# A two-layer transformer block on one core: both score tiles of a shared bank ahead of their passes, compressed scores and norms spread among dense steps, SBUF tiles at multiples of 128 bytes

## The chip, the core and the metric

One core of a Trainium2 chip runs the whole program in one launch. TensorE (PE) multiplies, VectorE (DVE) and ScalarE (ACT) do the elementwise work and the exponentials, GpSimd (POOL) does a few scalings, SyncE (SP) issues the DMAs. The metric is the device time of one execution in microseconds, as the median of several runs.

## The reference

Two transformer blocks run one after the other on one sequence of 512 tokens with a model width of 1024 in fp32. The first block is a gated FFN, then a mixer (sparse attention in the NSA manner with a compressed branch and two further branches, a gated convolution, attention to a memory of other tokens, merged by gates), then a second FFN. The second block has two layers, stick-breaking attention and "forgetting" attention, each followed by a gated FFN and a gated per-layer embedding. The two attentions that the change touches compute, for 16 heads of 64:

```python
# forgetting attention, per block of queries (second_block, layer 2)
logits = einsum('bhqd,bhkd->bhqk', qb, k) * scale + fb[..., :, None] - f_cum[:, :, None, :]
probs  = softmax(where(kpos <= tpos, logits, -inf), axis=-1)
out    = einsum('bhqk,bhkd->bhqd', probs, v)
# k and q are rms-normed per head; f_cum = cumsum(log_sigmoid(hs @ w_f + b_f))

# NSA mixer: o = g_cmp * attn(q, compressed k, v) + g_a * attn_a(q, k_a, v_a) + g_b * attn_b(q, k_b, v_b)
# with a relative bias per head and gates g = sigmoid(h @ w_g)
```

## The kernel before

All matrix products are fp32 split into a high and a low part, so that one product of 128 rows by 128 columns by 512 tokens is three matmuls (`mm3`). A dense projection of one 128-wide slice of outputs from 1024 inputs is eight such triples, 24 matmuls of 512 columns; in the kernel's words one triple is a *step* and eight steps are a *job*. A job fetches its weights (SP's queue, 512 KB), ACT makes the high part `wh`, DVE the low part `wl`; the pool `wp` keeps three sets, so the fetch runs a job or two ahead. `h0h`, `h0l` ... are the high and low parts of the normed activations, `u..` those of the FFN's hidden layer, `m..` those of an attention's output.

The program runs in stages, in the order of time: an FFN (90 to 426 us), memory attention (to 563), the NSA mixer (`nsa`, 563 to 1157), its merge (to 1235), an FFN (to 1545), stick-breaking attention (1600 to 1905), an FFN with the embedding (to 2310), forgetting attention (`forget`, pool "fox", to 2650), and a last FFN with the embedding. In an FFN every matmul is a step of a dense job.

An attention is worked in *units*, one head and one branch at a time (32 units in `nsa`, 16 in `forget`). In `unit_scores` the 512 by 512 scores are made in four tiles of 128 queries, of which tile i has (i+1)*128 keys. Tiles 0 and 1 share one PSUM bank (256 columns each, tag "s"), tiles 2 and 3 have one each; tag "s" has two banks. After each tile a *pass* on DVE (`softmax_rows`) adds the bias and takes the extremum per row, and ACT takes the exponential. Two dense steps stand ahead of tile 3. POOL scales the rows (`unit_scale`). In the next round `unit_turn` transposes the unit's probabilities on PE (tag "t"), ACT and DVE split them into `pth` and `ptl`, and `unit_out` multiplies them with V (tag "o").

So a unit is a chain across PE, DVE, ACT and POOL, and what keeps PE busy meanwhile are dense steps. `begin(jobs)` sets up a list of jobs, `feed(n)` emits n steps of it, `pace(upto)` emits steps until a count is reached. In the loop over units `upto` rises evenly, so the steps are spread evenly over what is left of them. While `self.pinned` is set, PE keeps the order in which the code is written; else the scheduler may move instructions.

In `nsa` before its loop stand, as plain code: the queries' and keys' projections, the values, gates, head norms, `compress` (a generator of the compressed keys and values) and the compressed scores `nsa_cmp` (16 DMAs fetch a bias into `cp`, PE adds scores, transposes, softmax on DVE, ACT and POOL, transposed back). `nsa_cmp` has three parts, divided by `yield`. In the loop the second half of the queries is normed at u = 9 to 12, and two more `nsa_cmp` run at u = 13 to 15.

In `forget` a list of jobs `lead(u)` makes K, Q and V of four heads; `head_stats` and `head_norm` norm them, and `doubled` and `stacked` write the split halves `hv` and copy them with DMAs into `kd`, `kl`, `qs`, from which the scores are multiplied. A norm's matmuls multiply `hrh`, `hrl` with `selr` into tag "s". Line numbers below are those of the kernel before: L184 is a matmul, L189 a transpose, L203 and L213 the split's high and low part, L626 the pass, L628 the exponential, L1081 and L1097 are in `nsa_cmp`, L417 in `head_norm`, L477 and L478 in `fold_halves`, L1341 in `forget`.

Of the kernel before, what the change touches and what calls it, by code (L numbers as in the profile page):

```python
# [16 lines left out]
P = 128  # L17
# [145 lines left out]
class Net:  # L163
    def __init__(self, ctx, tc, a, out):
# [4 lines left out]
        self.tags = self.TAGS = ("d", "s", "t", "o")  # L169
        self.sb = ctx.enter_context(tc.tile_pool(name="sb", bufs=1))  # L170
# [396 lines left out]
    def constants(self):  # L567
# [12 lines left out]
        sq = self.t(sb, NSQ * P, "nrq", 2)[:, : 4 * P]  # L580
# [36 lines left out]
    def softmax_rows(self, pool, src, n, bias, stat, tag, bufs):  # L617

        nc = self.nc
        m = self.t(pool, 1, tag + "m", 8)  # L620
# [252 lines left out]
    def unit_scores(self, pool, b, q, k, bias, mask=None):  # L873

        st = self.t(pool, NT, "st", 4)
        pr, sc = [], {}
        both = self.bank("s")
        for i in range(NT):
            n = (i + 1) * P
            w = max(n, 256)  # L880
            qi = slice(i * P, (i + 1) * P)
            if i == 3:
                self.feed(2)
            sc = both[:, 256 * i : 256 * i + 256] if i < 2 else self.bank("s")
            self.scores(sc[:, :w], b, q, k, qi, slice(0, w), False, True, mask is None)
            if mask is not None:
                self.mm(sc[:, qi], self.ident_b, mask, start=False, stop=True)
            pr.append(self.softmax_rows(pool, sc[:, :n], n, bias(n), st[:, i : i + 1], f"pr{i}", 2))
        return pr, st
# [27 lines left out]
    def nsa(self):  # L917
        nc, tc = self.nc, self.tc
        with self.pool("nsa", "right") as pool:
# [7 lines left out]
            for cb in range(2):  # L927
                def evac(i, ps, cb=cb):
                    g = slice(4 * cb, 4 * cb + 4)
                    self.split(V[:, i, g, 0], V[:, i, g, 1], ps[:, :256].rearrange("p (g d) -> p g d", d=64), rT[:, i : i + 1])  # L930
                    if i % 2:
                        next(comp, None)
                self.dense_tok(self.a["w_v"][cb], self.h, NT, evac)

            G = self.t(pool, NT * 48, "G").rearrange("p (i c) -> p i c", c=48)
            pg = self.dbank()
            self.dense(pg, self.a["w_g"][0], self.h)
            gt = self.t(pool, S, "cv", 4)
            nc.vector.tensor_tensor(gt, pg, self.rB, op=ALU.mult)
            nc.scalar.activation(gt, gt, AF.Tanh, scale=0.5)  # L940
            nc.vector.tensor_scalar(gt, gt, 0.5, 0.5, op0=ALU.mult, op1=ALU.add)
            tp = self.bank("t")
            for i in range(NT):
                nc.tensor.transpose(tp[:, i * P : (i + 1) * P], gt[:, i * P : (i + 1) * P], self.ident)
            nc.vector.tensor_copy(G, tp.rearrange("p (i c) -> p i c", c=P)[:, :, :48])
            nc.vector.tensor_scalar(G[:, 0, :16], G[:, 0, :16], self.col("valid"), None, op0=ALU.mult)
# [4 lines left out]
            for j in range(4):  # L951
                ps = self.dbank()
                self.dense(ps, self.a["w_kv"][4 + j], self.h)
                k = self.t(pool, S, f"kx{j}") if j % 2 else self.t(pool, S, "cv", 4)
                nc.vector.tensor_tensor(k, ps, self.rB, op=ALU.mult)
                ks.append(k)
                next(comp, None)
            for _ in comp:
                pass
            st = self.head_stats(ks, self.sel64, 1)  # L960
            for j in range(4):
                self.head_norm(ks[j], j, 1, st, self.col("kg"))
# [464 lines left out]
```

## Time and profile before

| what | value |
|---|---|
| median of 3 runs | 3084.95 us (3083.20 to 3086.88) |
| the profiled execution | 3091.85 us |
| its span, first to last instruction | 3090.1 us |
| PE busy | 2950.9 us, 95% of the span |
| DVE, ACT, POOL busy | 1632.7, 1223.0, 245.7 us |
| chain that ended last, share of PE | 68% |
| DMA queue 1, share of 16 engines' span | 35.6% |
| HBM over the span | 100 GB/s |

The profiled execution was one of the runs on the chip with the recorder on. PE's busy time counts a matmul from its start to a modelled end, and successive matmuls overlap, so 95% busy is not 95% of what PE could do. The view by windows gives the busy time of each engine in a stretch; the view of waits gives, per releasing instruction, how long an engine was idle before an instruction that this release let go.

### The profile page before, as it was taken

The numbers are of one execution on the slowest core, as the hardware profiler recorded it, in microseconds if no ns is written. First come the engines' busy times: TensorE is split into PE (matmuls) and PEld (weight loads), VectorE is DVE, ScalarE is ACT, GpSimd is POOL, SyncE is SP. The second block draws the span as 40 slices with busy tenths as digits, with TensorE's granted clock in tenths as the row PEclk, the third lists the DMA queues.
The fourth block names the chain that finished last, engine by engine and source line by source line (L and its number), as shares of the span: only waits on it lengthen the run. The fifth ranks groups of instructions, "written<-read, shape, count | busy, mean of one in ns | idle before, by whom it ended". The sixth has DMA issues, their size and how long they took to land.

```text
span 3090.1 us, 37192 instructions
## 1 busy us (share of the span) xinstructions
PE 2950.9 (95%) x13873; PEld 2384.8 (77%) x13874; DVE 1632.7 (53%) x2718; ACT 1223.0 (40%) x2078; POOL 245.7 (8%) x361
## 2 busy tenths in 40 slices
PE   8999999997988999999999999999999888999999
PEld 7888887875766778888888877888877666788887
DVE  7434345674666655443348775343366555644334
ACT  6322234352554544222236564222243454422223
POOL 0000000001223320000000000000013321000000
PEclk9999999998999999999999999999999898999999
DMA  7322342343232235223343345223334334522332
GB/s 234 105 96 90 105 129 86 95 125 104 72 105 81 79 129 180 91 93 94 108 127 102 100 120 177 96 91 94 90 125 120 91 86 140 166 91 95 91 95 95
DMA packets 133230, 339.20 MB, mean 110 GB/s; under 512 B 17415, under 2 KB 30215, under 8 KB 133048
## 3 DMA queue, kind: packets, MB, share of 16 engines
q1 hardware_dynamic: 132376, 335.49, 35.6%
q10 hardware_dynamic: 672, 1.32, 0.4%
q8 instruction: 109, 1.79, 0.2%
q14 instruction: 73, 0.60, 0.1%
HBM read 279.82 MB, written 28.61 MB: 100 GB/s over the span
## 4 chain that ended last, share of the span: by engine, by line
PE 68%; DVE 6%; issue 3%; DMA 3%; ACT 2%; POOL 1%; SPq 0%; DVEq 0%; POOLq 0%; ACTq 0%
PE d L184 25%; PE s L184 14%; PE o L184 13%; PE t L184 11%; PE t L189 2%; DVE wl L213 1%; ACT wh L203 1%; DVE pr L626 1%; DMA xd<-qk 1%; DMA qk<-xd 1%; DVE ptl L213 0%; PE s L1246 0%; PE o L1256 0%; PE t L1246 0%; DVE cv L809 0%
## 5 line engine op out<-in xcount | busy, mean ns | idle before, releaser
L203 ACT ACTIVATE wh<-raw 128x1024 fp32r<-128x1024 f32 (+3 forms) x499 | 493.2, 989 | 1238.5 <-PE d L184 330.2
L213 DVE TENSOR_TENSOR wl<-raw,wh 128x1024 fp32r<-128x1024 f32 (+3 forms) x499 | 573.7, 1150 | 317.4 <-ACT wh L203 303.3
L893 POOL TENSOR_SCALAR pr<-pr,st 128x128 f32<-128x128 f32 x192 | 111.6, 599 | 331.3 <-DVE st L1341 142.2
L213 DVE TENSOR_TENSOR ptl<-t,pth 128x512 fp32r<-128x512 f32 x144 | 85.3, 596 | 32.9 <-ACT pth L203 30.1
L203 ACT ACTIVATE pth<-t 128x512 fp32r<-128x512 f32 x144 | 74.6, 521 | 70.1 <-PE t L189 69.7
L626 DVE CUSTOM_DVE_ANT_0 pr<-s,tb 128x128 f32<-128x128 f32 (+3 forms) x128 | 60.3, 488 | 72.9 <-PE s L184 51.3
L225 POOL TENSOR_TENSOR raw<-raw,cols 128x1024 f32<-128x1024 f32 x25 | 50.6, 2025 | 557.3 <-DMA xd<-x 477.9
L189 PE MATMUL t<-idn,pr 128*128 128x128 f32 x480 | 79.7, 282 | 4.7 <-DVE ptl L213 3.6
L189 PEld LDWEIGHTS t<-idn,pr 128*128 128x128 f32 x480 | 61.9, 145 | 25.4 <-DVE ptl L213 6.5
L184 PE MATMUL o<-ptl,V 128*128 128x512 f32 x192 | 59.8, 323 | 9.2 <-DVE ptl L213 8.7
L184 PE MATMUL s<-kd,qs 128*128 128x256 f32 (+1 forms) x64 | 28.5, 446 | 36.8 <-DMA qs<-hvl 20.1
L402 POOL MEMSET hrh<- 128x512 f32 (+2 forms) x10 | 4.7, 472 | 666.7 <-DVE wl L213 485.0
L184 PE MATMUL d<-h0h,wh 128*128 128x512 f32 x136 | 57.0, 419 | 0.1
L184 PE MATMUL d<-h7h,wh 128*128 128x512 f32 x136 | 56.9, 418 | 0.0
L512 ACT ACTIVATE ta<-ta 128x512 f32<-128x512 f32 x88 | 55.6, 633 | 3.0 <-DVE ta L511 2.9
L184 PE MATMUL d<-h2h,wh 128*128 128x512 f32 x136 | 56.5, 416 | 0.0
L184 PE MATMUL d<-h4h,wh 128*128 128x512 f32 x136 | 56.4, 414 | 0.0
L184 PE MATMUL d<-h6h,wh 128*128 128x512 f32 x136 | 56.3, 414 | 0.0
L184 PE MATMUL d<-h5h,wh 128*128 128x512 f32 x136 | 56.2, 413 | 0.0
L184 PE MATMUL d<-h3h,wh 128*128 128x512 f32 x136 | 55.9, 411 | 0.0
L184 PE MATMUL d<-h1h,wh 128*128 128x512 f32 x136 | 55.6, 409 | 0.0
L184 PE MATMUL o<-pth,V 128*128 128x512 f32 x192 | 55.5, 322 | 0.0
(2173 smaller groups left out, 8749.5 us busy)
## 6 DMA issues: line engine op xcount, KB each, us to landing
raw<-in_f_in_dram SPq DMA_DIRECT2D x176, 512.0 KB
raw<-in_f_out_dram SPq DMA_DIRECT2D x64, 512.0 KB
raw<-in_f_out_dram SPq DMA_DIRECT2D x32, 384.0 KB
raw<-in_w_mg_dram SPq DMA_DIRECT2D x24, 512.0 KB
raw<-in_w_cv_dram SPq DMA_DIRECT2D x24, 512.0 KB
xd<-x SPq DMA_DIRECT2D x32, 256.0 KB
x<-xd SPq DMA_DIRECT2D x32, 256.0 KB
raw<-in_w_pg_dram SPq DMA_DIRECT2D x16, 512.0 KB
```

What stands on the lines that cost most here:

```text
L184: i = self.nc.tensor.matmul(out, lhs, rhs, **kw)
L189: i = self.nc.tensor.transpose(out, src, self.ident)
L203: nc.scalar.activation(h, src, AF.Copy, scale=1.0 if scale is None else scale)
L213: eng.tensor_tensor(lo, src, hb, op=ALU.subtract)
L225: nc.gpsimd.tensor_tensor(v, v, gain.unsqueeze(2).to_broadcast([P, gain.shape[1], n]), op=ALU.mult)
L402: nc.gpsimd.memset(z.bitcast(F32), 0.0)
L512: nc.scalar.activation(ta, ta, AF.Silu)
L626: nc.vector.tensor_tensor_reduce(out=p, in0=src, in1=bias, op0=ALU.add, op1=ALU.min, scale=1.0, scalar=3e38, accum_out=m)
L893: self.nc.gpsimd.tensor_scalar(pr[i], pr[i], st[:, i : i + 1], 1.0, op0=ALU.mult, op1=ALU.mult)
```

## The change

There are five edits.

1. `unit_scores`: the tiles run in the groups (0, 1), (2), (3). Within a group all matmuls stand ahead of all passes, so that tile 1 is multiplied ahead of the pass on tile 0.
2. `nsa`: the keys' projections, the values and the gates become jobs of the list (47 jobs instead of 40, so 392 steps in all, with 16 in each `values` job, instead of 320). The head norms, the parts of `compress` and the first two `nsa_cmp` stand between feeds. `pinned` is set later, once step 104 is reached or passed. In the loop the second part of the last `nsa_cmp` comes a unit later.
3. `forget`: the list of jobs starts ahead of the small projection `w_ff` and of the transposes; of each four heads K and Q come first and V last; V has two buffers instead of three; the norms of a head pair come at u % 4 of 2 and 3, two units or more ahead of their use and after `forget_out`, instead of right before it; the pacing aims at 176 steps at u = 9.
4. `halves`: the tile pair `hv` has two buffers in `stick` and `forget`, still one in `nsa`.
5. `t()` rounds a tile's width in SBUF up to a multiple of 128 bytes, and a tile `edge` of 96 bytes per row is put at the right side; the four tiles of row extrema share one tag `sm`; the gates' transposes go through `tr`.

The instruction counts stay about the same (PE 13941 rows in the order before, 13942 in the order after).

```diff
+        self.edge = ctx.enter_context(tc.tile_pool(name="edge", bufs=1, side="right"))
+        self.edge.tile([P, 24], F32, name="edge", tag="edge")
...
     def t(self, pool, cols, tag, bufs=None, dt=F32, parts=P):
         self.uid += 1
-        return pool.tile([parts, cols], dt, name=f"{tag}_{self.uid}", tag=tag, bufs=bufs)
+        w = cols if pool is self.ps else -(-cols // 64) * 64 if dt == BF16 else -(-cols // 32) * 32
+        x = pool.tile([parts, w], dt, name=f"{tag}_{self.uid}", tag=tag, bufs=bufs)
+        return x if w == cols else x[:, :cols]
...
-        h, lo = self.pair(pool, "hv", bufs=1)
+        h, lo = self.pair(pool, "hv", bufs=self.hv)
...
-        for i in range(NT):
-            n = (i + 1) * P
-            w = max(n, 256)
-            qi = slice(i * P, (i + 1) * P)
-            if i == 3:
+        for tiles in ((0, 1), (2,), (3,)):
+            if tiles == (3,):
                 self.feed(2)
-            sc = both[:, 256 * i : 256 * i + 256] if i < 2 else self.bank("s")
-            self.scores(sc[:, :w], b, q, k, qi, slice(0, w), False, True, mask is None)
...
-            pr.append(self.softmax_rows(pool, sc[:, :n], n, bias(n), st[:, i : i + 1], f"pr{i}", 2))
+            sc = {i: both[:, 256 * i : 256 * i + 256] if i < 2 else self.bank("s") for i in tiles}
+            for i in tiles:
+                w = max((i + 1) * P, 256)
+                qi = slice(i * P, (i + 1) * P)
+                self.scores(sc[i][:, :w], b, q, k, qi, slice(0, w), False, True, mask is None)
...
+            for i in tiles:
+                n = (i + 1) * P
+                pr.append(self.softmax_rows(pool, sc[i][:, :n], n, bias(n), st[:, i : i + 1], f"pr{i}", 2))
...
-            jobs = [query(0, r) for r in range(4)] + self.conv(0, pool) + self.conv(1, pool)
+            jobs = [key(j) for j in range(4)] + [query(0, r) for r in range(4)] + [values(0), self.job(self.a["w_g"][0], self.h, gates), values(1)]
+            jobs += self.conv(0, pool) + self.conv(1, pool)
...
+            for k in range(4):
+                self.feed(8)
+                next(comp)
+            st = self.head_stats(ks, self.sel64, 1, fill=2)
+            self.feed(6)
+            for j in range(4):
+                self.head_norm(ks[j], j, 1, st, self.col("kg"))
+                self.feed(2)
...
             for b in range(2):
-                for _ in self.nsa_cmp(pool, 0, b, [qn[0, r] for r in range(4)], kc, G, pc):
-                    self.feed(5)
-            base, total = self.steps, 8 * len(jobs)
+                next(cmps[b])
+                self.feed(6)
+                for _ in cmps[b]:
+                    pass
+                if b == 0:
+                    next(cmps[1])
+                self.feed(6)
+            self.pace(8 * 12 + 8)
+            self.pinned = True
+            base = self.steps
...
+            self.begin(jobs)
+            self.feed(16)
             ps = self.dbank()
             self.dense(ps, self.a["w_ff"][0], self.h, gs)
...
-                jobs = [self.values(pool, self.a["w_fv"][u], rT, V, u, gs, 3)]
...
+                return jobs + [self.values(pool, self.a["w_fv"][u], rT, V, u, gs)]
...
-                if u % 4 == 3 and u < 15:
-                    kq[t + 1] = norm(t + 1, hst)
...
-                if u % 4 == 2 and u < 14:
-                    self.pace(48 * (u // 4 + 2))
+                if u % 4 == 1 and u < 13:
+                    self.pace(48 * (u // 4 + 1) + 32)
                     hst = self.head_stats(xs[u // 4 + 1], self.sel64, 1, pool=pool, tag="o", fill=2)
-                elif u % 4 == 0 and 0 < u < 16:
-                    kq[t + 1] = norm(t + 1, hst)
+                elif u % 4 in (2, 3) and u < 12:
+                    n = 2 * (u // 4) + u % 4
+                    kq[n] = norm(n, hst)
```

How PE's order moves is seen at three places. The first is a unit in the loop of `nsa`, from the scores' first tile to the fourth. The `s` tiles are the score banks (`s_6436` holds tiles 0 and 1), `k1d`, `k1l` and `q1s` keys and queries, `d<-h..,wh` dense steps. Before:

```order
L184 MATMUL s_6436<-k1l_993_5384,q1s_1066_5700 128x256
L184 MATMUL s_6436<-k1d_1024_5542,q1s_1066_5700 128x256 [waits DVE_49]
L184 MATMUL s_6436<-k1l_993_5384,q1s_1066_5700 128x256
L184 MATMUL s_6449<-k1d_1024_5542,q1s_1066_5700 128x384
L184 MATMUL s_6449<-k1l_993_5384,q1s_1066_5700 128x384
L184 MATMUL d_6431<-h1h_75,wh_6327 128x512
L184 MATMUL d_6431<-h1l_76,wh_6327 128x512
L184 MATMUL d_6431<-h1h_75,wl_6328 128x512
L184 MATMUL d_6431<-h2h_77,wh_6327 128x512
L184 MATMUL d_6431<-h2l_78,wh_6327 128x512
L184 MATMUL d_6431<-h2h_77,wl_6328 128x512
L184 MATMUL s_6462<-k1d_1024_5542,q1s_1066_5700 128x512 [waits DVE_49]
```

and now:

```order
L189 MATMUL s_6335<-k1l_834_4516,q1s_1012_5334 128x256
L189 MATMUL s_6335<-k1d_948_5015,q1s_1012_5334 128x256
L189 MATMUL s_6335<-k1l_834_4516,q1s_1012_5334 128x256
L189 MATMUL s_6348<-k1d_948_5015,q1s_1012_5334 128x384
L189 MATMUL s_6348<-k1l_834_4516,q1s_1012_5334 128x384
L189 MATMUL d_6330<-h1h_79,wh_6227 128x512
L189 MATMUL d_6330<-h1l_80,wh_6227 128x512
L189 MATMUL d_6330<-h1h_79,wl_6228 128x512
L189 MATMUL d_6330<-h2h_81,wh_6227 128x512
L189 MATMUL d_6330<-h2l_82,wh_6227 128x512
L189 MATMUL d_6330<-h2h_81,wl_6228 128x512
L189 MATMUL s_6361<-k1d_948_5015,q1s_1012_5334 128x512 [waits DVE_49,PE_49]
```

The second matmul of tile 0 stands first in each piece. Tile 1's first matmul has lost its wait on DVE. Tile 3's first matmul, behind the same six dense matmuls, still waits on DVE.

The second place is the border between two units of `forget`, where the keys `kd` and queries `qs` change to the next head pair. Before:

```order
L184 MATMUL o_19840<-pth_19800,V_18760 128x256 [waits Activation_49]
L184 MATMUL o_19840<-ptl_19801,V_18760 128x128
L184 MATMUL o_19840<-pth_19800,V_18760 128x128
L184 MATMUL s_19853<-kd_3739_19782,qs_3743_19794 128x256 [waits DMAHW2_49,DMAHW1_49,DMAHW0_49]
L184 MATMUL s_19853<-kl_3513_18690,qs_3743_19794 128x256 [waits DMAHW3_49]
L184 LDWEIGHTS bfc_148
L184 MATMUL s_19853<-bfc_148 128x128
L184 MATMUL s_19853<-kd_3739_19782,qs_3743_19794 128x256 [waits DVE_49]
L184 MATMUL s_19853<-kl_3513_18690,qs_3743_19794 128x256
L184 LDWEIGHTS bfc_148
L184 MATMUL s_19853<-bfc_148 128x128
```

and now:

```order
L189 MATMUL o_19570<-ptl_19530,V_18921 128x128
L189 MATMUL o_19570<-pth_19529,V_18921 128x128
L189 MATMUL s_19583<-hrh_19469,selr_151 128x512
L189 MATMUL s_19583<-hrl_19470,selr_151 128x512
L189 MATMUL s_19587<-hrh_19469,selr_151 128x512
L189 MATMUL s_19587<-hrl_19470,selr_151 128x512
L189 MATMUL s_19614<-kd_3604_19106,qs_3608_19117 128x256 [waits DMAHW6_49,DMAHW4_49,DMAHW7_49,DMAHW3_49,DVE_49]
L189 MATMUL s_19614<-kl_3502_18634,qs_3608_19117 128x256 [waits DMAHW0_49]
L189 LDWEIGHTS bfc_152
L189 MATMUL s_19614<-bfc_152 128x128
L189 MATMUL s_19614<-kd_3604_19106,qs_3608_19117 128x256
L189 MATMUL s_19614<-kl_3502_18634,qs_3608_19117 128x256
```

Before, the scores stand right behind the unit's output and wait for three DMA queues. Now a norm for a later head pair (`hrh`, `hrl` with `selr`) stands between, in two score banks, and the scores wait among others on DVE.

The third place is the second compressed scores ahead of or in the loop of `nsa`: `cp` is transposed into `t`, goes through its softmax on DVE, ACT and POOL, and is transposed back. Before, its second transposes (those that wait on Pool) follow 15 dense matmuls behind the first ones, of which the last three are here:

```order
L184 MATMUL d_5930<-h3h_79,wh_5840 128x512
L184 MATMUL d_5930<-h3l_80,wh_5840 128x512
L184 MATMUL d_5930<-h3h_79,wl_5841 128x512
L189 MATMUL t_5943<-idn_144,cp_5862 128x128 [waits Pool_49]
L189 MATMUL t_5943<-idn_144,cp_5862 128x128 x3
```

and now:

```order
L189 MATMUL s_5938<-k1d_948_5015,q0s_1000_5290 128x512 [waits DVE_49]
L189 MATMUL s_5938<-k1l_834_4516,q0s_1000_5290 128x512
L194 MATMUL t_5757<-idn_148,cp_5697 128x128 [waits DMAHW4_49,DMAHW3_49,DMAHW5_49,DMAHW2_49,DMAHW6_49,DMAHW1_49,DMAHW7_49,DMAHW0_49,DVE_49]
L194 MATMUL t_5757<-idn_148,cp_5697 128x128 x3
L194 MATMUL t_5799<-idn_148,cp_5697 128x128 [waits Pool_49]
L194 MATMUL t_5799<-idn_148,cp_5697 128x128 x3
L194 MATMUL t_5959<-idn_148,pr_1094_5845 128x128 [waits DVE_49,PE_49]
L194 MATMUL t_5959<-idn_148,pr_1096_5849 128x128
L194 MATMUL t_5959<-idn_148,pr_1099_5856 128x128
L194 MATMUL t_5959<-idn_148,pr_1106_5876 128x128
```

Now the second transposes stand right behind the first, with no dense step between, and behind the scores of the loop's second unit.

## Rows read from the trace of the kernel before

**Rows 1.** The page: its first lines, busy time of each engine.

```profile
span 3090.1 us, 37192 instructions
...
PE 2950.9 (95%) x13873; PEld 2384.8 (77%) x13874; DVE 1632.7 (53%) x2718; ACT 1223.0 (40%) x2078; POOL 245.7 (8%) x361
...
```

**Rows 2.** Windows by stage: busy us (x instructions) per engine, granted clock, DMA share.

```profile
...
563.00:700.00 137.00, 129.88 (x705) 106.57 (x704) 97.28 (x197) 57.24 (x81) 7.90 (x16) 1.00 0.40 120
700.00:770.00 70.00, 52.28 (x191) 38.96 (x190) 32.08 (x55) 19.04 (x30) 9.36 (x8) 0.83 0.35 99
770.00:1157.00 387.00, 346.90 (x1743) 280.93 (x1742) 241.51 (x556) 193.53 (x440) 112.35 (x154) 0.98 0.31 92
...
2310.00:2330.00 20.00, 15.70 (x98) 12.88 (x97) 16.96 (x25) 9.16 (x14) 7.35 (x7) 0.91 0.36 119
2380.00:2650.00 270.00, 222.54 (x1126) 175.12 (x1125) 160.65 (x336) 131.50 (x285) 58.29 (x80) 0.90 0.38 109
...
```

**Rows 3.** Waits of PE in nsa's loop, 770 to 1157: total, times, longest.

```profile
...
PE s L184 <- DVE pr0m L626: 22.7, 31, 1.6
PE o L184 <- DVE ptl L213: 8.2, 9, 1.9
PE t L189 <- DVE ptl L213: 3.1, 5, 1.7
PE t L189 <- DVE cp L1081: 3.0, 1, 3.0
...
```

**Rows 4.** Waits of PE in forget, 2310 to 2650.

```profile
...
PE s L184 <- DMA qs<-hvl: 20.1, 5, 5.4
PE s L184 <- DVE pr0m L626: 16.3, 15, 3.9
PE s L184 <- DVE st L1341: 5.2, 2, 3.1
...
PE s L184 <- DVE hrl L213: 1.6, 3, 1.3
...
PE s L184 <- DVE hrh L207: 1.2, 1, 1.2
...
```

**Rows 5.** Waits of PE ahead of nsa's loop, 563 to 770.

```profile
...
PE t L189 <- POOL cp L1097: 5.2, 2, 3.0
...
```

**Rows 6.** Timeline of a unit in nsa: start, length, engine, idle before and releaser.

```profile
...
812.96 0.28 PE L184 MATMUL s<-k1d,q1s 128*128 128x256 f32 x1
...
813.08 0.28 PE L184 MATMUL s<-k1l,q1s 128*128 128x256 f32 x1
...
814.87 0.39 PE L184 MATMUL s<-k1d,q1s 128*128 128x256 f32 x1 [1.51 <-DVE pr0m L626]
...
```

**Rows 7.** Timeline of the border between two head pairs in forget.

```profile
...
2512.96 0.28 PE L184 MATMUL o<-pth,V 128*128 128x128 f32 x1
2513.27 0.59 ACT L477 ACTIVATE on<-o 64x512 f32<-64x512 f32 x1 [1.22 <-PE o L184]
2513.90 0.68 DVE L478 TENSOR_TENSOR on<-o,on 64x512 f32<-64x512 f32 x1 [1.39 <-ACT on L477]
...
```

**Rows 8.** Windows inside long dense runs, PE alone: up, down, merge's projection.

```profile
...
154.00:174.00 20.00, 20.00 (x88) 1.00 0.28 84
345.00:365.00 20.00, 20.00 (x88) 1.00 0.42 115
1185.00:1205.00 20.00, 20.00 (x90) 1.00 0.68 251
...
```

**Rows 9.** Timeline of the second compressed scores.

```profile
...
755.36 0.63 PE L189 MATMUL t<-idn,cp 128*128 128x128 f32 x4 [1.47 <-DVE cp L1081]
...
760.55 1.05 POOL L1097 TENSOR_TENSOR cp<-cp,cz 128x512 f32<-128x512 f32 x1 [0.25 <-DVE cz L1096]
...
761.66 1.12 PE L189 MATMUL t<-idn,cp 128*128 128x128 f32 x4 [2.17 <-POOL cp L1097]
...
```

**Rows 10.** Window around the longest wait in forget, PE alone.

```profile
...
2514.00:2528.00 14.00, 8.87 (x33) 0.63 0.21 52
...
```

More of the change, by code (lines that the diff above doesn't have):

```diff
@@ L926, in nsa, with values, evac, gates @@
             V = self.t(pool, NT * 1024, "V", dt=F32R).rearrange("p (i g z d) -> p i g z d", g=8, z=2, d=64)
-            for cb in range(2):
-                def evac(i, ps, cb=cb):
+            def values(cb):
+                def evac(i, ps):
                     g = slice(4 * cb, 4 * cb + 4)
                     self.split(V[:, i, g, 0], V[:, i, g, 1], ps[:, :256].rearrange("p (g d) -> p g d", d=64), rT[:, i : i + 1])
-                    if i % 2:
-                        next(comp, None)
-                self.dense_tok(self.a["w_v"][cb], self.h, NT, evac)
+                return self.job_tok(self.a["w_v"][cb], self.h, NT, evac)
             G = self.t(pool, NT * 48, "G").rearrange("p (i c) -> p i c", c=48)
[L936 to L946, printed above, removed]
+            def gates(pg):
+                gt = self.t(pool, S, "cv", 4)
+                nc.vector.tensor_tensor(gt, pg, self.rB, op=ALU.mult)
+                nc.scalar.activation(gt, gt, AF.Tanh, scale=0.5)
+                nc.vector.tensor_scalar(gt, gt, 0.5, 0.5, op0=ALU.mult, op1=ALU.add)
+                tp = self.bank("t")
+                for i in range(NT):
+                    self.tr(tp[:, i * P : (i + 1) * P], gt[:, i * P : (i + 1) * P])
+                nc.vector.tensor_copy(G, tp.rearrange("p (i c) -> p i c", c=P)[:, :, :48])
+                nc.vector.tensor_scalar(G[:, 0, :16], G[:, 0, :16], self.col("valid"), None, op0=ALU.mult)
             kc = [self.t(pool, 4 * P, f"kc{z}", dt=F32R) for z in range(4)]
@@ L950, in nsa, with key, post @@
             ks = []
[L951 to L962, printed above, removed]
+            def key(j):
+                def post(ps):
+                    k = self.t(pool, S, f"kx{j}") if j % 2 else self.t(pool, S, "cv", 4)
+                    nc.vector.tensor_tensor(k, ps, self.rB, op=ALU.mult)
+                    ks.append(k)
+                return self.job(self.a["w_kv"][4 + j], self.h, post)
             los = [self.zeroed(pool, f"k{br}")[0] for br in range(2)]
@@ L1018, in nsa @@
                     next(cmp0)
-                elif u == 15:
-                    next(cmp1)
                 if rows:
@@ L1041, in nsa @@
                 elif u == 15:
+                    next(cmp1)
+                    kn[1] = keys(1, 1)
+                elif u == 16:
                     next(cmp1, None)
-                    kn[1] = keys(1, 1)
                 self.pace(upto)
@@ L1336, in forget @@
                 t, b = u // 2, u % 2
[L1337 to L1338 removed]
+                upto = base + (176 - base) * (u + 1) / 10 if u < 10 else 176 + 46 * (u - 9) / 7
                 if u < 16:
```

69 lines of the change are left out of this document (39 added, 30 removed).

## The prediction, made before the changed kernel ran

> **What bounds the kernel now.** I read the page first. PE is busy 95% of a span of 3090.1 us, DVE 53%, ACT 40% [rows 1]; PE is the engine that sets the end, so a gain must come from PE's idle time or from matmuls that take less. The profiled execution took 3091.85 us, 1.75 us more than its span; all sums below are made against it. The median of the three runs is 3084.95, which is 6.9 lower, and I take the same 6.9 off at the end.
>
> Then I asked by windows where PE isn't busy. Inside the long dense runs 20 of 20 us are busy at clock 1.00 [rows 8]. What is idle lies in the two attentions with filler: ahead of the loop of `nsa` 137.0 - 129.88 + 70.0 - 52.28 = 24.8 us, in its loop 40.1, at the start of `forget` 4.3 of 20, in the rest of it 47.5 [rows 2]. That is 117 us, and the change's edits 1 to 4 lie in these stretches. The view of waits then names what ended that idle time [rows 3 to 5].
>
> **Edit 1, tile 1 ahead of the pass on tile 0.** In the loop of `nsa` PE's wait for that pass costs 22.7 us in 31 times [rows 3], in `forget` 16.3 in 15 [rows 4]. The idle time is counted from the modelled end of the matmul before. Unhindered, a 256-column score matmul follows the one before at 813.08 - 812.96 = 0.12 us though each is 0.28 long [rows 6]; so a wait also loses the overlap of 0.16. This makes 22.7 + 31 x 0.16 = 27.7 and 16.3 + 15 x 0.16 = 18.7, together 46.4. In the new order tile 1 has no wait. Late next is tile 3, which takes the bank that tiles 0 and 1 shared, and waits for the pass on tile 1. Between stand tile 2 and six dense matmuls, about 1.7 us; the two passes now begin one tile later (two matmuls, 0.24 us) and are in sum under 1 us. So tile 3 finds its bank free except where DVE is held by something longer; I count 0.05 us per unit, 48 units, 2.4 back. Sum: -44. Bounds: -46.4, and -20 if tile 3 gets back more than half of it.
>
> **Edit 2, ahead of the loop.** Of the 24.8 us, the named waits are the chains of code that had no steps beside them; the largest kind is the compressed scores' wait for POOL, 5.2 in two [rows 5]. With steps in between most go. Two things come back. The second compressed scores' transposes now stand right behind each other. Their softmax chain runs on DVE, ACT and POOL from 755.36 + 0.63 to 761.66, 5.7 us [rows 9]; before, 15 dense matmuls covered most of it, and now nothing does, so 5.7 us. The first scores and the remaining short waits I count at 5, two waits of 2.5 or their like. Sum: -24.8 + 5.7 + 5 = -14. Bounds: -24.8, and +2: three chains of 5.7 uncovered, 17.1, and 10 of the old waits left. The 16 DMAs that fill `cp` wait on SP for the first scores to be done with the tile, and weights are queued behind them; `wp` holds two jobs more, 11 us of steps, so I count nothing for it.
>
> **Edit 2, in the loop.** The list is longer, so of it some 272 steps are left for 32 units by my count of the order, 8.5 in each, where there were 244, 7.6. The 0.9 step more is 0.9 x 3 matmuls of about 0.23 us, 0.6 us of cover per unit. It stands against waits for `ptl` of 8.2 + 3.1 us in 14 times [rows 3], 0.8 each. Each could lose 0.6, 8.4 in all; as the step isn't always put between transposes and output, I take half, -4.5 (bounds 0 and -8.4). The wait for `cp` in the loop, 3.0 [rows 3], gets a unit more: -2 (0 and -3). The steps themselves cost nothing new: they are the same matmuls that stood ahead of the loop. What it costs DVE: 241.5 us busy in the loop of 387 [rows 2], 62%; with 28 steps, 3.5 jobs, more in it and some 45 us less of time it comes to 71%, still not the bound.
>
> **Edit 3.** At the start of `forget` 4.3 us are idle [rows 2]; two jobs' steps now stand ahead of the small projection, -4 (0 and -4.3). In the loop the queries' DMAs cost 20.1 us in five waits; the norm's waits for score banks and for `hrh`, `hrl` cost 5.2 + 1.6 + 1.2 = 8.0 [rows 4]. The norms now come two units ahead, so the DMAs have a whole unit, 270 / 16 = 17 us [rows 2]; the second buffer of `hv` (edit 4) takes away the wait of one norm's split for the other's DMAs. 28.1 go. What is new: six norms in the loop stand right behind the unit's output and take both score banks, and the next unit's tile 0 waits for the norm's pass on DVE, which is queued behind the output's own `on`. That chain: the last output matmul ends at 2512.96 + 0.28 = 2513.24, `on` on ACT and then DVE ends at 2513.90 + 0.68 = 2514.58 [rows 7], the norm's pass on 512 columns is another 0.7 like `on`, so PE waits 2.0 us, six times 12. No dense step stands between. Sum: 12 - 28.1 = -16. Bounds: -28, and +2 if the passes on the next tile 0, queued behind the norm's three splits of 0.7 each, hold up tile 3 as well and the wait is 5 us a time. The V buffer that goes is needed again only after the units that read it: nothing.
>
> **The clock.** Where PE waits long, the granted clock falls: 0.63 in 2514 to 2528, around the longest wait of 5.4 us, where 33 instructions took 14 us [rows 4, 10]. The means are 0.83 in 700 to 770, 0.98, 0.91 and 0.90 [rows 2]. Had PE been the bound all that time, busy x (1 - clock) would be given back: 8.9 + 6.9 + 1.4 + 22.3 = 39.5. Much of what ran slowly only met its next wait sooner or later, and the new waits of 2 to 6 us will bring some of it back: I take a fifth, -8 (0 and -39.5).
>
> **Edit 5.** No row shows the same tile at another address. What the rows show is that dense runs of one form differ: 88 matmuls in 20 us where `h` or `u` moves, 90 where merge's `m` does, all at clock 1.00 and with PE never idle [rows 8]. That is 227.3 against 222.2 ns by these counts, 5.1 ns each, with one count more or less 2.5 to 7.7. In the built program merge's `m` and its `wh` start at the same residue modulo 512 bytes, while `h` or `u` and `wh` do not; with the new widths `u` and `wh` share one (384), `h` (256) and `wh` still don't. If that relation is the cause, `u`'s 4 x 8 x 22 x 3 = 2112 matmuls gain 10.8 us. It rests on one run that differs, so I take two thirds, -7. Bounds: 0, and some 8700 moving matmuls of `h` and `u` x 5.1 = -44.
>
> The Trainium skill speaks against this term: in "TensorE: Matmul & The Clock Gate", "Step-by-step: what each phase is for", the moving and the stationary operand have a read port each, and "Loading the next tile's weights doesn't steal SBUF read bandwidth from the running matmul", so addresses of one against the other shouldn't matter. By that rule the term is 0 and the time 7 us later; the trace's 90 against 88 doesn't agree by itself.
>
> **Sum.** -44 - 14 - 4.5 - 2 - 4 - 16 - 8 - 7 = -99.5; 3091.85 - 99.5 = 2992.35, less 6.9 is 2985.
>
> **Rivals.**
> *The waits only move.* PE is released from tile 1 and meets tile 3, the norms' passes and the uncovered `cp` chain at their bounds: -20 + 2 - 2 + 2 = -18, with nothing from clock or addresses. For it speaks that a unit is one chain over four engines, each of which was waiting; against, that DVE is busy only 62% in the loop [rows 2]. Time 3085 - 18 = 3067; halfway to the forecast is 3026.
> *All dense matmuls run at the rate of merge's.* -44 instead of -7: 2948. For it speaks the one run at 90; against, that only `u` gets the relation which that run has.
> *The edits don't do what they say.* If the scheduler or the pools put the same waits back, the time stays 3085. Against it stands the new order itself, in which tile 1 has no wait.
> *Slower, by the clock.* Each of 48 units now has its wait at tile 3, behind the dense steps. If that wait, or the one after the norm, is as long as those of `forget` now, the clock falls in each unit, as around 2514 [rows 10]. PE's 346.9 + 222.5 = 569 us busy in both loops stand at a mean near 0.95 now [rows 2]; at mean c they take 569 x (0.95/c - 1) more. The forecast's gain is used up at c = 0.81; at 0.78 it is +124, so 3085 - 100 + 124 = 3109. Against it: tile 3's cover of 1.7 us is longer than the two passes.
>
> **Chances.** The forecast, with the terms near their taken values (2960 to 3010): 0.60. Dense matmuls at merge's rate: 0.10. Waits that move in part or whole: 0.22. No change: 0.03. Slower by the clock: 0.05. A measurement can tell about 0.2%, 6 us, from no change. So faster 0.91, same 0.04 (the third rival and the edge of the first), slower 0.05. The range goes from 2935 (the second rival with some more clock) to 3040 (the first, three quarters of it).
>
> **What would show it.** Right: no row of waits "s <- DVE pass" at tile 1, tile 3's in its place under 3 us in sum; no wait for `qs<-hvl` in `forget`, waits of about 2 us six times for the norm's pass; one wait near 5.7 us for `cp` from POOL near the loop's start; clock over 0.95 in `forget`; `u` at 90 per 20 us and `h` at 88. Wrong: tile 3 waiting half a microsecond in most units; a weights fetch ending PE's idle time; 88 everywhere in the long runs (the addresses do nothing), or 90 everywhere.

## The result, and the profile after

The changed kernel takes 2971.41 us (median of 4 runs, 2970.22 to 2973.13) where the kernel before took 3085.91 (median of 4, 3083.20 to 3090.15) beside it: a ratio of 0.9628, 95% interval 0.9612 to 0.9645, 114.5 us less. The forecast was 2985 with a range of 2935 to 3040.

The page of the changed kernel's profiled execution, busy time of each engine over the span, answers to [rows 1]:

```profile
span 2971.2 us, 37172 instructions
...
PE 2898.9 (98%) x13873; PEld 2369.6 (80%) x13874; DVE 1628.5 (55%) x2718; ACT 1216.9 (41%) x2078; POOL 247.9 (8%) x361
...
```

The span is 118.9 us shorter, PE's busy time 52. So a bit more than half of the gain, 67 us, is PE's idle time that went, and the rest is time in which PE counts as busy: matmuls at a higher clock, or at the same clock from a better place, and overlaps that a wait had broken.

The windows of the same places of the program (busy us and instructions of each engine, granted clock) answer to [rows 2]: ahead of the loop of `nsa`, its loop, and `forget`'s start and loop.

```profile
...
559.00:696.00 137.00, 123.06 (x644) 99.73 (x644) 94.37 (x183) 58.69 (x81) 6.91 (x14) 1.00 0.40 119
696.00:722.00 26.00, 23.24 (x134) 19.64 (x134) 19.21 (x41) 8.05 (x14) 3.19 (x2) 0.97 0.50 145
...
722.00:1105.00 383.00, 365.63 (x1863) 302.08 (x1862) 255.79 (x583) 200.37 (x456) 116.69 (x158) 0.98 0.35 102
2247.00:2267.00 20.00, 17.67 (x72) 12.98 (x71) 17.41 (x19) 8.50 (x11) 10.28 (x10) 1.00 0.37 121
2267.00:2307.00 40.00, 38.26 (x207) 32.03 (x205) 29.95 (x38) 17.96 (x26) 13.28 (x8) 0.96 0.43 122
2307.00:2507.00 200.00, 186.59 (x1091) 151.43 (x1090) 143.89 (x305) 116.91 (x263) 63.24 (x76) 0.98 0.45 126
...
```

Ahead of the loop of `nsa` PE is idle for 16.7 us (24.8 before), in the loop for 17.4 of 383 (40.1 of 387 before), and in that of `forget` for 13.4 of 200 (47.5 of 270, a window that ends some 20 us behind the last scores), where the granted clock is 0.98 instead of 0.90.

The waits of PE, in the loop of `nsa` (first fence, answers to [rows 3]) and in `forget` (second, to [rows 4]): total, times, longest. `sm` is the tile of row extrema that a pass writes, formerly `pr0m` and so on.

```profile
...
PE t L194 <- POOL cp L1128: 4.7, 1, 4.7
PE s L189 <- DVE sm L631: 4.0, 5, 1.0
PE t L194 <- DVE cp L1112: 3.6, 2, 2.9
PE t L194 <- DVE ptl L218: 2.3, 3, 1.4
PE o L189 <- DVE ptl L218: 1.7, 2, 1.2
...
```

```profile
...
PE s L189 <- DVE x L422: 5.2, 9, 2.1
PE s L189 <- DVE sm L631: 4.2, 4, 1.9
PE o L189 <- DVE ptl L218: 3.9, 7, 1.1
...
```

No tile 1 waits any more. What is left of the pass is 4.0 + 4.2 us: in `nsa` three times at tile 2 and twice at tile 3, in `forget` four times at tile 3. The queries' DMAs are gone from the list in `forget`; the norm's pass (`x`, L422) has come in for 5.2, and the wait for `ptl` has grown from 0.5 + 0.5 to 3.9. In `nsa`, the 4.7 for `cp` from POOL is the compressed scores' chain, which stood ahead of the loop before and now lies in it.

Where the time went, by the stretches of the program, from the starts of the first and last matmuls of each in the traces (us; the columns of the experiments are explained below):

| stretch | before | after | unit scores alone | widths alone | nsa alone | forget alone |
|---|---|---|---|---|---|---|
| four FFN second halves, sum | 490.3 | 477.9 | 490.3 | 477.9 | 489.8 | 490.3 |
| end of FFN 1 to first unit of nsa | 324.4 | 290.1 | 325.2 | 326.2 | 290.1 | 324.0 |
| units of nsa | 352.3 | 338.3 | 321.8 | 351.6 | 372.1 | 351.7 |
| end of FFN 3 to first unit of forget | 134.5 | 117.2 | 134.4 | 133.8 | 134.7 | 118.6 |
| units of forget | 243.5 | 199.5 | 219.1 | 240.6 | 239.8 | 221.8 |
| behind them to FFN 4's second half | 278.6 | 284.0 | 278.2 | 277.2 | 278.2 | 284.1 |
| whole span | 3090.1 | 2971.2 | 3035.4 | 3070.6 | 3068.1 | 3058.1 |

A stretch that an edit doesn't touch moves by up to 4 us from one execution to the next (units of `forget` in the column "nsa alone"), so smaller differences say nothing.

### The profile page after: what moved, and what is told of

Read it like the earlier page. It is cut to its first block, busy times and chain, and to the rows that moved or that the text cites. A ratio compares the mean times of both kernels' runs of the same rounds, so it can differ in the third digit from the quotient of the medians.

```text
span 2971.2 us, 37172 instructions
## 1 busy us (share of the span) xinstructions
PE 2898.9 (98%) x13873; PEld 2369.6 (80%) x13874; DVE 1628.5 (55%) x2718; ACT 1216.9 (41%) x2078; POOL 247.9 (8%) x361
## 4 chain that ended last, share of the span: by engine, by line
PE 72%; DVE 5%; issue 3%; ACT 1%; DMA 1%; POOL 0%; SPq 0%; DVEq 0%; POOLq 0%; ACTq 0%
PE d L189 27%; PE s L189 14%; PE o L189 14%; PE t L189 12%; PE t L194 2%; DVE wl L218 1%; DVE cv L814 1%; DMA qk<-xd 0%; DVE ptl L218 0%; DMA xd<-qk 0%; PE s L1278 0%; PE o L1288 0%; PE t L1278 0%; PE o L1289 0%; ACT wh L208 0%
## 5 line engine op out<-in xcount | busy, mean ns | idle before, releaser
L633 ACT ACTIVATE pr<-pr,sm 128x128 f32<-128x128 f32 x192 | 106.0, 553 | 64.1 <-DVE sm L631 63.6
L518 DVE TENSOR_TENSOR ta<-s,ta 128x512 f32<-128x512 f32 x22 | 15.2, 692 | 74.6 <-PE s L189 74.6
L518 DVE TENSOR_TENSOR ta<-t,ta 128x512 f32<-128x512 f32 x22 | 15.2, 692 | 74.1 <-PE t L189 74.0
L482 ACT ACTIVATE on<-o 64x512 f32<-64x512 f32 x48 | 28.6, 595 | 65.8 <-PE o L189 51.1
```

The lines of the kernel that those rows point to most:

```text
L482: self.nc.scalar.activation(dst[h], po[64:], AF.Copy)
L518: nc.vector.tensor_tensor(ta, pb, ta, op=ALU.mult)
L633: nc.scalar.activation(p, p, AF.Exp, bias=m, scale=-1.0, accum_out=stat)
```

## The experiments

**One edit at a time.** Four kernels, each the kernel before with one group of edits.

```diff
 e1_unit:  before + edit 1 (unit_scores of the changed kernel)
 e5_width: before + edit 5 (t(), edge, sm, sq)
 e2_nsa:   before + edit 2 (nsa's body)
 e34_fox:  before + edits 3 and 4 (forget's body, hv buffers)
```

> The kernel before with edit 1 alone (both score tiles of a bank multiplied ahead of their passes). Theory, the wait for the pass on tile 0 was the loss and is not replaced: 31 waits in nsa and 15 in forget go, 44 us faster, some 27 of it between the start of the compressed scores and the merge and some 17 in forget, and tile 3 waits under 3 us in sum in each of the two. Rival, the unit is one chain and the wait moves to tile 3 or to ptl: 20 us faster or less, with tile 3 waiting half a microsecond in most units.

Measured 3037.15 us, ratio 0.9836 (0.9821 to 0.9850). The units of `nsa` are 30.5 us shorter, those of `forget` 24.4. PE's waits in the loop of `nsa` in this kernel:

```profile
...
PE o L184 <- DVE ptl L213: 9.3, 10, 1.9
PE t L189 <- DVE ptl L213: 5.8, 6, 2.0
...
PE s L184 <- DVE pr1m L626: 1.1, 2, 0.8
...
```

The pass's 22.7 us [rows 3] became 1.1, and `ptl` went from 11.3 to 15.1. So some 4 us moved to the next wait in the chain, and the rest was gained; the rival falls. In `forget` tile 3 waits 1.4 us in this kernel, twice. `forget` got more than its waits' 17 us, with the granted clock going from 0.90 to 0.95:

```profile
...
2360.00:2585.00 225.00, 194.68 (x1066) 155.37 (x1065) 142.69 (x308) 116.97 (x264) 56.74 (x77) 0.95 0.40 114
...
```

> The kernel before with edit 5 alone (tile widths rounded to 128 bytes, the edge tile, the shared tag sm). Theory, a 512-column matmul is faster when its moving tile and the weights loaded beside it start at the same residue modulo 512 bytes: only the FFNs' second halves gain, 2112 matmuls by 5 to 6 ns, 11 to 13 us, 3 in each FFN; the stages with h moving stay. Rival 1, a multiple of 128 bytes is what counts, as the rounding says: h gains as well, 40 us or more. Rival 2, two read ports, addresses do nothing: within 3 us of before.

Measured 3074.62 us, ratio 0.9957 (0.9942 to 0.9972). Each FFN's second half takes 119.5 us instead of 122.5 or 123.0, as in the changed kernel, and the other stretches of the table don't move beyond what executions differ by. The theory holds so far, and both rivals fall: `h` doesn't gain, and the 12 us by the medians are not nothing.

> The kernel before with edit 2 alone (nsa's keys, values and gates as jobs, norms and compressed scores between feeds, the unit's scores as before). Theory, the steps cover waits ahead of the loop and the longer list covers ptl in it: 20 us faster (14 ahead of the loop, 6 in it); nothing outside nsa moves. Rival, the steps taken out from ahead of the loop and the uncovered softmax chain of cp leave new holes: under 8 us.

Measured 3070.80 us, ratio 0.9946 (0.9931 to 0.9961). Ahead of the units it gains 34.3 us, and in the units it loses 19.8. 28 steps of 0.70 us went from ahead of the units, 27 of them into the units by the trace, 18.9 us; so the gain ahead is 34.3 - 19.6 = 14.7 net, and the units gain nothing. The waits in the loop show why:

```profile
...
PE s L184 <- DVE pr0m L626: 26.3, 32, 2.3
PE t L189 <- POOL cp L1120: 5.4, 1, 5.4
PE s L184 <- DVE pr1m L626: 3.6, 4, 1.6
PE o L184 <- DVE ptl L213: 3.0, 2, 1.9
PE t L189 <- DVE ptl L213: 1.0, 3, 0.5
...
```

`ptl` fell from 11.3 to 4.0, and the 3.0 for `cp` from DVE [rows 3] are gone. Two things took that back: the passes rose by some 6 us (half of that at tiles 2 and 3, `pr1m`, mostly in the first two units), and the compressed scores' chain, which stood ahead of the loop before, is uncovered in it for 5.4. So the split of the theory, 14 ahead and 6 in the loop, is not what the stretches show; 14.7 and nothing is, with the chain's wait counted in the loop.

> The kernel before with edits 3 and 4 alone (forget's lead order, norms two units ahead, two hv buffers). Theory, the DMA waits for qs go and six new waits of 2 us for the norm's pass come: 20 us faster, plus up to 8 of clock. Measured for forget as a whole in the changed kernel was 56, of which edit 1 has some 17 by the waits' count, so 30 to 40 here would say that the six waits are smaller than forecast or that the clock gives back more; 20 or less that edits 1 and 3 need each other.

Measured 3059.31 us, ratio 0.9906 (0.9889 to 0.9922). By stretches -15.9, -21.7 and +5.5, so -32.1: the upper case of the two, the edits don't need each other (24.4 + 32.1 = 56.5 against the 55.9 of both). 17 steps less stand ahead of the units by the order (78 before, 61 now), 11.9 us; by the trace three of them run in the units and fourteen behind, where the stretch grew by only 5.5. So the start itself gains 4.0 and the rest 21.7 + 11.9 - 5.5 = 28.1, some 24 of it in the units. While tile 1 still waited, the norm's pass itself cost 1.1 us, but the wait for the pass on tile 0 rose from 16.3 [rows 4] to 21.8:

```profile
...
PE s L184 <- DVE pr0m L626: 21.8, 16, 5.2
...
```

**Edit 2 taken out of the whole.** The changed kernel with the old body of `nsa`.

```diff
-    def nsa(self):   # of the changed kernel
+    def nsa(self):   # of the kernel before, with hv at one buffer
```

> The changed kernel without edit 2 (nsa's body as before, with tile 1 ahead of the pass and the rounded widths). Theory, edit 2 gains 14.5 us alone and some 3 more with edit 1 there, as the waits for ptl that edit 1 makes longer (15 us in the kernel with edit 1 alone, 11 before) are covered by the longer list: 18 us slower than the changed kernel. Rival, the edits just add: 14 slower, with ptl waits near 11.

Measured 2996.03 us, ratio 0.9706 (0.9689 to 0.9724). In the stretches of `nsa` it is 35.2 - 16.4 - 0.7 = 18.1 us slower; the rest of the 24 lies in stretches that the edit doesn't touch. PE's waits for `ptl` in its loop:

```profile
...
PE o L189 <- DVE ptl L218: 9.3, 10, 1.9
...
PE t L194 <- DVE ptl L218: 6.0, 6, 2.0
...
```

They are 15.3 us, against 4.0 in the changed kernel, so the rival's sign, waits near 11, isn't there, and the theory's is. By the time the two can't be told apart: 18.1 and the 14.5 of edit 2 alone differ by less than a stretch moves from one execution to the next.

**The address.** Four kernels on the changed one. In it the weights lie at 384 modulo 512 bytes, `u` at 384, `h` at 256.

```diff
 h_same: zb's tile (128 bytes) allocated ahead of h instead of behind
+        zero = self.t(sb, 2, "zb", dt=BF16)
         self.h = [self.pair(sb, f"h{c}") for c in range(KC)]
 w_moved: the same, and eps in a spare column of cols (all of it 128 bytes lower)
 u_sweep, in ffn() behind the hidden layer's tiles:
+            pad = {"f1": 8, "f2": 16, "f3": 64, "f4": 120}[name]
+            pool.tile([P, pad], F32, name=f"pad_{name}", tag="pad")
 h_256: eps in a spare column of cols, and a 128-byte pad behind rB
```

> The changed kernel with one 128-byte tile (zb) moved in SBUF from behind the h tiles to ahead of them, so that h starts at 384 modulo 512 bytes as wh and wl do; all other addresses and the order stay. Theory, the same residue modulo 512 of the moving tile and of the weights loaded beside it is what gains: some 6400 matmuls of h by 5.8 ns, 37 us faster than the changed kernel, about 2934; the FFN up stretches go from 88 matmuls per 20 us to 90. Rival, it is something in the FFN's second half (another PSUM pattern, less traffic) and not the residue: within 3 us of 2971.

Measured 2942.33 us (2936.52 to 2944.35), ratio 0.9537 (0.9521 to 0.9553). That is 29 us below the changed kernel by the medians and 36.6 by the spans of the profiled executions (2934.6 against 2971.2); the theory's 37 holds by the second and is somewhat high by the first. The profiled execution is the shortest of its four. The rival falls by either.

> The changed kernel with the weights moved instead: h stays at 256, wh and wl come to 256, u stays at 384 modulo 512 (eps goes into a spare column of cols, zb ahead of h). Theory, the relation counts: h gains 37 us, u loses its 12.5, in sum 25 faster than the changed kernel, about 2947, each FFN's second half back at 122.5 us. Rival, 384 is a good residue by itself, for the moving tile: u stays fast, h slow, 2971. Rival, 384 good for the weights: all slow, 2984.

Measured 2952.93 us, ratio 0.9570 (0.9556 to 0.9584), 18 us below the changed kernel where the theory had 25. Each FFN's second half is at 123.0, and where `h` moves it is as fast as in h_same: the first FFN's second half begins at 308.4 us, in h_same at 308.5 and in the changed kernel at 314.8. So the relation counts, not the place; of the missing 7 us, 5.6 are in the units of `forget` (202.1 us against 196.5 in h_same), for which nothing here gives the cause.

> The changed kernel with u moved by another pad in each FFN: weights minus u is 32 bytes in the first FFN, 64 in the second, 256 in the third, -32 in the fourth (modulo 512), 0 in the changed kernel. Theory, only 0 is fast: each FFN's second half goes from 119.5 back to 122.5 us, 12 us slower in all. Rival, a multiple of 256 is enough: the third stays at 119.5. Rival, 64 is enough: the second and the third stay.

Measured 2985.64 us in one run. The second halves take 123.0, 123.0, 119.5 and 123.0. The theory's 512 fails: 256 off is as good as 0.

> The changed kernel with h at 128 modulo 512 bytes (eps in a spare column of cols, a 128-byte pad behind rB) and the weights still at 384, so 256 apart. In the sweep the one FFN in which u was 256 off stayed fast. Theory, 256 bytes is the period: as fast as with h at 384, 35 us faster than the changed kernel, 90 matmuls per 20 us. Rival, the period is 512 and the sweep's third FFN was something else: 2971.

Measured 2938.54 us, ratio 0.9521 (0.9501 to 0.9541), the fastest of all and not to be told from h_same. With `h` too, 256 bytes apart is as good as 0.

PE alone in windows of 20 us within long dense runs, in the changed kernel (first `h`, then `u`), in h_same (`h`), in w_moved (`h`, then `u`), in u_sweep (`u` in the first and the third FFN) and in h_256 (`h`):

```profile
...
154.00:174.00 20.00, 20.00 (x87) 1.00 0.26 86
345.00:365.00 20.00, 20.00 (x90) 1.00 0.47 136
...
```

```profile
...
154.00:174.00 20.00, 20.00 (x90) 1.00 0.34 106
...
```

```profile
...
154.00:174.00 20.00, 20.00 (x90) 1.00 0.34 105
345.00:365.00 20.00, 20.00 (x87) 1.00 0.36 104
...
```

```profile
...
345.00:365.00 20.00, 20.00 (x87) 1.00 0.43 116
...
2110.00:2130.00 20.00, 20.00 (x90) 1.00 0.31 87
...
```

```profile
...
154.00:174.00 20.00, 20.00 (x90) 1.00 0.31 106
...
```

90 where the two tiles start a multiple of 256 bytes apart, 87 where they don't, all at clock 1.00 and with PE busy throughout. A second half has 528 such matmuls, and from the start of the first to that of the last are 527 of their lengths: 119.5 against 122.5 to 123.0 us is 226.8 against 232.4 to 233.4 ns each, 5.7 to 6.6 ns.

**Which part of `forget`'s edits removed the DMA wait.** Three kernels on the changed one: the norms in their old places, one `hv` buffer, and both.

```diff
 norm_late
-                elif u % 4 in (2, 3) and u < 12:
-                    n = 2 * (u // 4) + u % 4
-                    kq[n] = norm(n, hst)
+                elif u % 4 == 0 and 0 < u < 16:
+                    kq[t + 1] = norm(t + 1, hst)
...
+                if u % 4 == 3 and u < 15:        # ahead of unit_turn
+                    kq[t + 1] = norm(t + 1, hst)
 hv1_early, in forget
+        self.hv = 1
 hv1_late: both
```

> The changed kernel with forget's norms back in their old places (at u % 4 of 3 between scores and turn, and of 0 behind the output), so right before their use for every other one; the rest of edits 3 and 4 stays. Theory, the place of the norms is what edit 3 gains in the loop: the waits for qs come back in three to six borders at 3.5 to 5 us and with them a low clock there, 15 to 25 us slower. Rival, the second hv buffer is the gain, since a norm's DMAs held up the next split: within 5 us of 2971.

> The changed kernel with one hv buffer in forget instead of two; the norms stay two units ahead. Late norms with two buffers (norm_late) cost nothing, so the place of the norms alone was not the gain. Theory, either the earlier place or the second buffer is enough to hide the queues' DMAs: within 5 us of 2971 here. Rival, the second buffer alone is the gain: 15 to 25 us slower.

> The changed kernel with one hv buffer in forget and the norms in their old places. Theory, either one is enough and without both the wait for qs is back: four to six waits of 3 to 5 us, 15 to 25 us slower than the changed kernel. Rival, neither matters, the waits went by the order K and Q first or the earlier statistics: within 5 us of 2971.

| | two hv buffers | one |
|---|---|---|
| norms two units ahead | 2971.41, ratio 0.9628 (0.9612 to 0.9645) | 2977.01, 0.9647 (0.9627 to 0.9667) |
| norms in the old places | 2970.06, 0.9624 (0.9609 to 0.9638) | 2988.69, 0.9684 (0.9666 to 0.9702) |

The expectation of norm_late, that the place is the gain, fell: with two buffers the old places cost nothing. Without both, 17 us come back. PE's waits in `forget`, with both undone, with the late norms alone and with one buffer alone: 15.6 us for the queries' DMAs in the first, 1.9 in the second, 4.8 in the third.

```profile
...
PE s L189 <- DMA qs<-hvl: 11.7, 4, 4.9
...
PE s L189 <- DMA qs<-hvh: 3.9, 1, 3.9
...
```

```profile
...
PE s L189 <- DMA qs<-hvl: 1.9, 1, 1.9
...
```

```profile
...
PE s L189 <- DMA qs<-hvh: 4.1, 1, 4.1
...
PE s L189 <- DMA qs<-hvl: 0.7, 1, 0.7
...
```

The 4 us for `qs<-hvh` are the wait of the very first unit, and both kernels with one buffer have it: their stretch ahead of the units is 5 us longer (122.6 and 122.2 against 117.2). There only the buffer helps. Within the units either one is enough: 198.9 us with one buffer and early norms, 196.6 with two buffers and late norms, 199.5 with both, 211.4 with neither.

The timeline of the kernel before, around the wait of 5.40 us for `qs<-hvl`, shows what the buffer does: start, length, engine, idle before and its releaser.

```profile
...
2508.67 0.74 DVE L417 SCALAR_TENSOR_TENSOR x<-x,cols,s 128x512 f32<-128x512 f32 x1
2508.79 0.63 ACT L203 ACTIVATE hvh<-x 128x512 fp32r<-128x512 f32 x1 [1.57 <-DVE x L417]
...
2509.45 0.47 SPq L457 DMA_DIRECT2D kd<-hvh  x1
...
2514.41 0.63 ACT L203 ACTIVATE hvh<-x 128x512 fp32r<-128x512 f32 x1 [0.55 <-DMA kd<-hvh]
...
```

The queries' norm was done at 2508.67 + 0.74 = 2509.41, yet their split into `hvh` began at 2514.41, 5.0 us later, when the DMAs that read the keys' `hvh` from the same buffer had landed.

## Why the prediction was right, step by step

The time fell in the range, and the waits that edits 1 and 3 were to remove did go. But the nearness is in part luck: less idle time went than the terms for the waits add up to (67 us against 44 - 7.4 of lost overlap + 14 + 4.5 + 2 + 4 + 16 = 77), and more came from the clock and from the addresses. The forecast was 14 us short by the medians and 19 by the profiled executions (99.5 against 118.9 by their spans), to which the figures by stretches below belong.

*Edit 1* was put at -44. Alone it took 49 us by the medians and 55 by the spans, 30.5 of it in `nsa` and 24.4 in `forget`. What comes back at tiles 2 and 3, put at 2.4, is 1.1 + 1.4 with edit 1 alone. In the changed kernel it is 8.2: there edits 2 and 3 put other work of DVE ahead of some passes, and tile 3 alone waits 5.2, more than the "under 3 us in sum" that was to show the forecast right. What exceeds the 44 has a likely cause in the clock, 0.90 to 0.95 in `forget`, which the working counted as a separate, small term.

*Ahead of the loop*, -14: measured -14.7, and that is luck. The idle time there went from 24.8 to 16.7: the first scores and the "remaining short waits" were counted at 5 and are three times that, and the chain put at 5.7 comes on top, in the loop. What made up for it is the clock, whose mean in the last stretch before the loop went from 0.83 to 0.97; by the working's own measure, busy time x (1 - clock), that gives back 8.9 - 0.7 = 8.2 us, an estimate. The largest waits that went are not the 5.2 for POOL that the working named, but those for the queries' DMAs, 9.0 us in three in the kernel before:

```profile
...
PE s L184 <- DMA q2s<-hvl: 4.2, 1, 4.2
PE s L184 <- DMA q3s<-hvl: 2.5, 1, 2.5
...
PE s L184 <- DMA q1s<-hvl: 2.3, 1, 2.3
...
```

The new wait that the order showed is there, but behind the scores of the loop's second unit, so that it counts in the units' stretch and not here; the second compressed scores' transposes in the timeline of the changed kernel:

```profile
...
740.09 0.66 PE L194 MATMUL t<-idn,cp 128*128 128x128 f32 x4 [2.95 <-DVE cp L1112]
745.45 1.12 PE L194 MATMUL t<-idn,cp 128*128 128x128 f32 x4 [4.70 <-POOL cp L1128]
...
```

The chain of 745.45 - 740.09 - 0.66 = 4.7 us is uncovered, forecast as 5.7.

*In the loop*, -4.5 and -2 for `ptl` and `cp`: nothing in the stretch with edit 2 alone, where the chain's 5.4 and the passes took back what `ptl` and `cp` gave; with edit 1 in place `ptl` falls from 15.3 to 4.0, more than forecast. `cp` from DVE did not fall in the changed kernel (3.0 before, 3.6 now). For the whole of edit 2 it is 18.1 us beside edit 1, against the 20.5 forecast.

*Edit 3.* The start was -4, and is 4.0. In the loop -16 was forecast and 28.1 measured with the clock's part in it. The step that failed is what the new order costs, "PE waits 2.0 us, six times 12": it comes to 5.2 in nine waits for the norm's pass, and only one of them is 2 us long. The border between two units in the changed kernel, PE and DVE from the norm's matmuls to the next unit's tile 3, and one instruction of POOL:

```profile
...
2405.66 0.45 PE L189 MATMUL s<-hrh,selr 128*128 128x512 f32 x1
...
2406.38 0.75 DVE L422 SCALAR_TENSOR_TENSOR x<-x,cols,s 128x512 f32<-128x512 f32 x1 [1.28 <-PE s L189]
2406.41 0.40 PE L189 MATMUL s<-hrl,selr 128*128 128x512 f32 x1
2407.16 0.68 DVE L483 TENSOR_TENSOR on<-o,on 64x512 f32<-64x512 f32 x1
...
2407.18 0.38 PE L189 MATMUL s<-kd,qs 128*128 128x256 f32 x1 [0.38 <-DVE x L422]
...
2408.45 1.90 POOL L230 TENSOR_TENSOR raw<-raw,cols 128x1024 f32<-128x1024 f32 x1 [3.12 <-DMA raw<-in_w_fv_dram]
2408.54 2.35 DVE L218 TENSOR_TENSOR hvl<-x,hvh 128x512 fp32r<-128x512 f32 x1
...
2408.67 0.45 PE L189 MATMUL s<-kd,qs 128*128 128x384 f32 x1 [0.55 <-DVE x L422]
...
2412.01 0.28 DVE L631 CUSTOM_DVE_ANT_0 pr<-s,fb 128x128 f32<-128x128 f32 x1
...
2412.79 0.47 PE L189 MATMUL s<-kd,qs 128*128 128x512 f32 x1 [1.95 <-DVE sm L631]
...
```

Two things were left out. The norm has four matmuls of its own on PE, from 2405.66 to 2406.41 + 0.40 = 2406.81, which cover the first microsecond; and here DVE takes the norm's first pass ahead of `on`, not behind it. What PE waits for the norm's passes is 0.38 and 0.55. In one of the six, at 2347.63, DVE is busy with two weight splits and `on` first, and there the wait is 2.11. The working had also said that no dense step stands in between, six times; by the order that is true of four.

What the sum left to its upper bound does happen: the passes on the next unit's tiles queue behind the norm's splits and hold up tile 3. All four waits of tile 3 in `forget`, 4.2 us, stand in units right behind a norm, so the new order's cost is 5.2 + 4.2 = 9.4 us, near the 12 but made up otherwise. Here tile 0's pass begins at 2412.01 and tile 3 waits 1.95. In three of the four cases a split of the norm took 2.35 to 2.38 us where the usual one takes 0.68, each begun just behind the start of a scaling of fetched weights on POOL (2408.45 for 1.90 here); the working has no such term.

Of the two reasons that the step gave for the DMA waits to go, the norms' earlier place and the second `hv` buffer, either is enough within the units; only the buffer does it for the first unit.

*The clock*, -8, is the term that was most mis-sized: the mean went from 0.90 to 0.98 in `forget`, in the loop of `nsa` it stayed at 0.98. Edit 1 alone brings `forget` to 0.95. By the working's own formula the 39.5 us fell to 0.7 + 7.3 + 1.5 + 3.7 = 13.2 with the rows of the changed kernel, so 26 us came back, not a fifth of 39.5. This is an estimate: each run removed the waits along with the low clock, and none shows the clock's part alone. It would lie in the 11 and the 12 us by which edits 1 and 3 exceed their terms, and in what was gained ahead of `nsa`.

*Edit 5*, -7, was 2112 x 5.1 = 10.8 with two thirds of it counted: measured -12.4 by the four second halves. The relation was the right one, the weight given to it too small, and its period wrong: 256 bytes, not 512. The rule of two read ports in the Trainium skill ("TensorE: Matmul & The Clock Gate", "Step-by-step: what each phase is for"), as the prediction applied it to addresses, would have had 0 here; seven kernels with the two tiles at different distances measure 6 ns a matmul.

The rivals: "the waits only move" is worth 4 us of `ptl` in `nsa` with edit 1, 8.2 us at tiles 2 and 3 in the changed kernel, and all of the loop's gain in edit 2 alone. "All dense matmuls at merge's rate" was not this change, but h_same and h_256 made it so: 29 and 33 us by the medians, 36.6 and 33.4 by the spans, where the bound was 44 - 11 = 33 for `h`. "Slower, by the clock" had waits at tile 3 in six units of 48, and the granted clock rose all the same.

## What to carry to other kernels

Where two tiles share a PSUM bank, write both before anything reads either; PE waited for that in 46 of 48 units, and the edit alone was worth 49 us. Steps that fill one wait of a chain pay only as far as the next wait doesn't grow: 28 steps more took 7 us from the waits for `ptl`, and the passes and an uncovered chain gave them back. When a forecast comes out right, add up its idle time and its clock apart, as here the one was too high and the other too low. Put the moving and the stationary tiles of long matmul runs a multiple of 256 bytes apart in SBUF; it costs one moved tile, and with `h` and `u` so this kernel takes 2938.54 us, a ratio of 0.9521 (0.9501 to 0.9541).

## What the runs showed of the hardware

A 512-column fp32 matmul in a run of them, each with a new stationary tile, took 226.8 ns (119.5 us by 527) where the moving tile and the weights started a multiple of 256 bytes apart, and 232.4 to 233.4 ns where they were 32, 64 or 128 bytes off such a multiple, at clock 1.00. For `h` it made no difference whether the pair lay at 384 modulo 512 bytes (h_same) or at 256 (w_moved). The cause within the chip isn't shown; no run separated the weight load from the matmul.

The mean granted clock in `forget` was 0.90 with 20.1 us of waits for the queries' DMAs (up to 5.4 each) and 16.3 for the pass (1.1 each on average), 0.95 when edit 1 alone had taken the latter away, and 0.98 with all edits, where no single wait is longer than 2.1 us.

A split of 128 x 512 on DVE that usually takes 0.68 us took 2.35 to 2.38 in four cases in `forget` of the changed kernel (one of them ahead of the units), each begun while POOL scaled 128 x 1024 fetched weights for 1.9 to 2.0 us.
